# Products of rounded operands that take their columns in four turns of four, in a two-block transformer kernel

## The chip, the cores and the metric

The kernel runs on one core of a Trainium2 chip. The metric is the device time of one execution in microseconds. The engines are called by the profile's names: PE is the matrix engine (PEld its weight loads, which overlap its products), DVE the vector engine, ACT the scalar engine, POOL the general one, SP the one that issues the transfers.

## The reference, cut to what matters

256 tokens of width 1024 pass through two blocks in float32. The first block has latent attention, a state space, cross attention and a convolved gated feed-forward; the second has two layers of a gated feed-forward, a mixer with three branches, and another gated feed-forward. Nearly all arithmetic is in dense products with weights that are read once:

```
x = x + 0.5 * ((silu(h @ w1) * (h @ w3)) @ w2)          # four times, w1 and w3 1024 x 2816, w2 2816 x 1024
proj = h @ w_in[l]                                       # 1024 x 5632, two layers
merged = gate_0 * (y_sb @ w_sb) + gate_1 * (y_ret @ w_ret) + gate_2 * (y_pool @ w_pool)
x = x + merged @ w_out[l]
```

## The kernel before, in words

A float32 product is made of three products of rounded operands. `split` writes a value's high part (type float32r, by ACT) and the rest (float32r, by DVE); names that end in h and l are these parts (`wh`, `wl` of the weights, `gh`, `gl` of the gated values), and `h` is the normed input, in the two parts. `mm3` adds high by high, high by low and low by high into one PSUM bank. Products that aren't of such operands (transposes, attention, the state space) stay plain float32.

There are two forms. In `proj`, the down products and `merge_out` (tiles `pr`, `up`, `acc`) the tokens are the 128 columns of the stationary operand and 512 columns of weights stream through (some `pr` have 256, 160 or 384). In `proj_T` (tiles `pt`) the weights are stationary and both token tiles stream, 256 columns: the moving operand is a view `p t c` of two runs of 128. In `h` these two runs lie 512 elements apart, since `norm_T` lays a tile out as token tile, block, column (`t k c`); `split_pairs` does the same for the gated values of a first chunk. The output bank is written in the same order as the columns stream.

All instructions are recorded first, with estimated costs, and `Program.issue` gives each engine its order by a list schedule. What depends on what is found in `add`: two accesses to a tile depend on each other where `region` says that they overlap. `region` gives the box from an access's first to its last element of a row. PSUM banks count as whole. The schedule's own estimates are not used as times in this text.

All `mm` calls go through line 463, all transposes through line 488, ACT, DVE and POOL operations through line 379.

Of the kernel before, what the change touches and what calls it, by code (L numbers as in the profile page):

```python
# [18 lines left out]
D = 1024  # L19
# [23 lines left out]
def region(ap):  # L43
    """The partitions and the elements of a row that an access path may touch."""
    (row, parts), *free = ap.ap
    p, f = divmod(ap.offset, row)
    lo = f + sum(min(0, s * (n - 1)) for s, n in free)
    hi = f + sum(max(0, s * (n - 1)) for s, n in free) + 1
    return p, p + parts, lo, hi


def overlap(a, b):
    return a[0] < b[1] and b[0] < a[1] and a[2] < b[3] and b[2] < a[3]


def covers(a, b):
    return a[0] <= b[0] and b[1] <= a[1] and a[2] <= b[2] and b[3] <= a[3]


class Op:  # L60
    """An instruction to come: its engine, its call and its estimated time."""
# [7 lines left out]
class Program:  # L69
    """Records instructions with their data's order and issues them by a list schedule.  # L70

    Per engine, the instruction that is ready and comes first by priority goes next, as long
    as the rest of the program can still run in the order of an earlier schedule within the
    tile pools. The priorities are start times of the schedule that runs from the end.
    """

    ENGINES = ("pe", "act", "dve", "pool", "sp")
    # time from the end of an instruction to the start of one on another engine that waits for it
# [19 lines left out]
    def tile(self, t, tags, whole=False):  # L98
        """Makes a tile known: the pools it takes room in, and if any two accesses keep their order."""
        name = t.tensor.name  # L100
        self.tags[name] = tags
        if whole:
            self.whole.add(name)
        return t

    def add(self, eng, call, cost, reads, writes, kind=""):
        op = Op(eng, call, cost, kind)
        # the vector engine's second port to SBUF is Pool's only one
# [4 lines left out]
        for aps, w in ((reads, False), (writes, True)):  # L113
            for ap in aps:
# [5 lines left out]
                r = (0, 1, 0, 1) if name in self.whole else region(ap)  # L120
# [23 lines left out]
    def backward(self, order):  # L144
        """Latest start times, from a schedule that runs from the end, later instructions of order first."""
# [42 lines left out]
    def forward(self, prio, base):  # L188
        """A schedule by priority; base is an order that keeps within the pools."""
# [32 lines left out]
        def room(i, full):  # L222
            """The tiles that op i takes into use, or None when there is no room for them."""
# [126 lines left out]
class Engine:  # L350
    """An engine's calls, recorded with their cost."""
# [33 lines left out]
class Ctx:  # L385
    """Pools, constants, and the blocks shared by all layers."""
# [43 lines left out]
    def weights(self, w, n0, n):  # L430
        """w[:, n0:n0+n] as the two float32r parts of a product, per 128-row block a list of (hi, lo)."""
# [25 lines left out]
    def mm(self, ps, lhsT, rhs, start=True, stop=True):  # L457
        n, m = size(rhs), size(lhsT)
        if rhs.dtype == F32:
            ns = 2 * max(2 * n / 2.4 * min(1.0, 0.4 + m / 160), 107.0 * m / 128) + 5  # L460
        else:
            ns = max(n, 64) / 2.4 + 2.5
# [3 lines left out]
    def mm3(self, ps, x, w, start, stop):  # L466
        """ps (+)= x.T @ w, the small product of the low parts left to float32's rounding."""
        self.mm(ps, x[0], w[0], start, False)
        self.mm(ps, x[0], w[1], False, False)
        self.mm(ps, x[1], w[0], False, stop)  # L470

    def mm_rows(self, ps, xs, ws, start, stop):
        """ps[i] (+)= sum over k of xs[k].T @ ws[i][k], the products with the low parts of x last."""
# [23 lines left out]
    def split(self, src, hi, lo, scale=None):  # L497
        """Splits float32 data into two float32r parts, scaled by a constant or per partition."""
# [14 lines left out]
    def transposes(self, src, name="tr"):  # L513
        """[128, 128 n] to a bank with the n blocks transposed."""
# [11 lines left out]
    def load_gain(self, src, kind="load"):  # L526
        """A gain vector of 1024, on all partitions."""
# [5 lines left out]
    def norm_rows(self, halves, g):  # L533
        """rmsnorm of [128, 1024] rows given as two halves."""
        ss = self.sm("ss", 2)
        xs = [self.w("xs") for _ in range(2)]
        for b in range(2):
            junk = self.w("junk")
            # D is an even power of two: the scale is exact
# [10 lines left out]
    def norm_T(self, tiles, g):  # L550
        """rmsnorm of 256 rows, transposed and split: per half of the width (hi, lo), each [128, 2, 4, 128]."""
        out = []
        for b in range(2):
            pair = [self.prog.tile(self.hpool.tile([128, 1024], F32R, tag="h", name="h"), ("h",)) for _ in range(2)]
            out.append([v.rearrange("p (t k c) -> p t k c", t=2, k=4) for v in pair])
# [6 lines left out]
    def split_tokens(self, ps, dst, t):  # L562
        """Splits [128, 4 * 128] into the columns of token tile t of dst."""
# [3 lines left out]
    def norm_x(self, gain):  # L567
        """The norm of both token tiles of x, for the products to come."""
# [10 lines left out]
    def proj(self, w, n0, n, x=None, rows=False):  # L579
        """x.T @ w[:, n0:n0+n], per token tile; with rows one tile after the other."""  # L580
# [19 lines left out]
    def proj_T(self, w, n0, x=None):  # L600
        """w[:, n0:n0+256].T @ x for all tokens: two blocks of 128 rows in a bank."""
# [14 lines left out]
    def merge_out(self, m, scale, w):  # L616
        """x += (scale * m).T @ w, m as four tiles of two 128-row blocks of all tokens."""
# [16 lines left out]
    def swiglu(self, w1, w3, w2):  # L634
        """x += 0.5 * (silu(h w1) * (h w3)) w2."""
# [22 lines left out]
    def conv_swiglu(self, w_up, w_down, cw, cb):  # L658
        """x += (silu(g) * v) w_down with [g | v] the causal convolution of h w_up along the tokens."""
# [39 lines left out]
    def feed_forward(self, w1, w3, w2, gate_rows, gate, scale):  # L699
        """x += scale * gate(h w1, h w3) w2, by chunks of the inner width.  # L700

        The first chunk takes the token tiles one after the other, as the norm hands them over."""
# [43 lines left out]
    def gate_proj(self, w, n0, bias=None):  # L746
        """Gate of one branch, two blocks of 128 rows to a tile; with half the bias, tanh of half the logits."""
# [14 lines left out]
    def branch(self, y, w, gate, m, plus_one):  # L762
        """m + gate * (w.T @ y), into the gate's tiles when m is None."""
# [10 lines left out]
    def head_sums(self, src, heads, dim):  # L774
        """Sums of squares over the last axis of [128, heads, dim]; src may lie in PSUM."""
# [6 lines left out]
    def head_norm(self, src, heads, dim):  # L782
        """1 / rms over the last axis of [128, heads, dim]; src may lie in PSUM."""
        return self.rstd(self.head_sums(src, heads, dim), heads, dim)

# [1 line left out]
    def rope_tables(self):  # L787
        """cos and sin of positions * inv_freq, [128, 2, 16] each, from the reduced angles."""
# [12 lines left out]
    # 2 pi in parts of few bits, so that their products with the turns are exact  # L801
    PI2 = (6.28125, 0.0019340515136718750, 1.2556659e-06)

    def reduce_angle(self, ang, shift):
        """ang - 2 pi k, k = round(ang / 2 pi + shift)."""
# [20 lines left out]
    # The state space runs in chunks of 4 steps, a step's number being 4 a + b, with the inputs and the  # L826
    # outputs in the order (b, a). With s the state before a chunk and d the factor of a step (complex):
    #   output b of the chunk = sum over b' <= b of (C d^(b - b') B) u[b'] + (C d^b) g,  g = d s
    #   g of the next chunk   = d^4 g + sum over b of (d^(4 - b) B) u[b]
    # and in a frame that turns with the angle of d^4 the second is a scan with a real decay.  # L830

    def ssm_setup(self):
        """Powers of the factors, the angles of whole chunks, and the input and output maps."""
# [28 lines left out]
        # k - w with k = round(w + 1/4)  # L862
# [8 lines left out]
        # powers 0..4 of the factors  # L871
# [4 lines left out]
        # (factor - 1) / lambda  # L876
# [15 lines left out]
        # its products with the powers 4, 3, 2, 1, 0  # L892
# [15 lines left out]
    def ssm_maps(self, h):  # L908
        """Maps of state tiles 8h .. 8h + 8, block diagonal by the two groups of a tile."""
# [4 lines left out]
        def product(x, y, signs, powers, name):  # L914
            """x (real, imaginary), [128, i, c], by powers of y [128, z, k, i]; per part and four tiles [128, i, k, 32]."""
# [23 lines left out]
        # C[1] holds the negative imaginary part  # L939
# [15 lines left out]
        # cos and sin of the angles of 1..64 chunks  # L955
# [16 lines left out]
    def ssm_half(self, h):  # L972
        """The outputs of state tiles 8h .. 8h + 8."""
# [44 lines left out]
    def ssm_gelu(self):  # L1018
        # 2 gelu(y) = y (1 + tanh(sqrt(2 / pi) (y + 0.044715 y^3)))
# [11 lines left out]
    def ssm_glu(self):  # L1031
        """y * sigmoid(y @ w_glu + b_glu), with the width on the partitions."""
# [23 lines left out]
    def softmax(self, s, heads, scale):  # L1056
        """Over the last axis of [128, heads, n] in a bank."""
# [13 lines left out]
    def cross_T(self, src, g):  # L1071
        """Per-head rmsnorm of [128, 4 * 128] rows, transposed per head."""
# [31 lines left out]
    def split_pairs(self, ps, dst, t):  # L1104
        """Splits [128, n * 128] into token tile t's part of each (hi, lo) of dst, two blocks to one."""
        for i, d in enumerate(dst):
            q = size(d[0]) // 2
            self.split(ps[:, i * 256:i * 256 + q], *(z[:, t * q:t * q + q] for z in d))

    def pair_T(self, ys):  # L1110
        """Accessor for [128, 2 * 256] tiles that hold two 128-row blocks of all tokens."""
        return lambda k: tuple(v[:, (k % 2) * 256:(k % 2) * 256 + 256].rearrange("p (t c) -> p t c", t=2) for v in ys[k // 2])

    def tile_T(self, ys):
        """Accessor for the tiles of split_pairs."""
        return lambda k: tuple(v.rearrange("p (t k c) -> p t k c", t=2, c=128)[:, :, k % 2, :] for v in ys[k // 2])

    def mla_latents(self, t, cq, ckv, g, out):
        """Norms of the latents, transposed and split; rotated shared key part per token tile."""
# [8 lines left out]
        # shared key part: its sum of squares and its rotation, gains folded into the tables  # L1128
# [9 lines left out]
    def fold_rope(self, sn, cs, gb):  # L1138
        """Rotation tables with the gains of the rotated dims folded in, per token tile."""
# [20 lines left out]
    def mla_heads(self, qs, kv, lat, gq, gk):  # L1160
        """Four heads: norms, rotation, causal softmax, values: [128, 2 * 256], split."""
# [23 lines left out]
        # first token tile: own keys only; later keys of the own tile get the mask added  # L1185
# [401 lines left out]
```

## Time and profile before

| | |
|---|---|
| time, median of 3 runs | 1622.44 us (1622.29 to 1624.53) |
| span of the profiled execution | 1619.3 us |
| instructions | 28502 |
| PE busy, products | 1589.3 us, 98%, 11126 records |
| PEld busy, weight loads | 1455.3 us, 90% |
| DVE, ACT, POOL busy | 1019.0, 843.1, 134.9 us |
| HBM read | 284.88 MB, 177 GB/s over the span |
| granted PE clock | 0.998 of full |

The span is the time from the first to the last instruction of one profiled execution; the time of a run lies some 3 us above it. A product's duration in the profile runs from its start to the modelled end of its last column, so products that follow each other closely overlap; how fast they go is read from starts, or from a stretch's length over its count. A plain float32 product leaves two records, one of rounded operands one.

### The profile page before, as it was taken

The numbers are of one execution on the slowest core, as the hardware profiler recorded it, in microseconds if no ns is written. First come the engines' busy times: TensorE is split into PE (matmuls) and PEld (weight loads), VectorE is DVE, ScalarE is ACT, GpSimd is POOL, SyncE is SP. The second block draws the span as 40 slices with busy tenths as digits, with TensorE's granted clock in tenths as the row PEclk, the third lists the DMA queues.
The fourth block names the chain that finished last, engine by engine and source line by source line (L and its number), as shares of the span: only waits on it lengthen the run. The fifth ranks groups of instructions, "written<-read, shape, count | busy, mean of one in ns | idle before, by whom it ended". The sixth has DMA issues, their size and how long they took to land.

```text
span 1619.3 us, 28502 instructions
## 1 busy us (share of the span) xinstructions
PE 1589.3 (98%) x11126; PEld 1455.3 (90%) x11126; DVE 1019.0 (63%) x1759; ACT 843.1 (52%) x1746; POOL 134.9 (8%) x276
## 2 busy tenths in 40 slices
PE   7999999999999999999999999999999999999998
PEld 6889989899989999889998999899998899989997
DVE  6678797787676545755657554665457556574543
ACT  6984554665555434555446443454345554464431
POOL 4554500000000000000000000000000000000000
PEclk9999999999999999999999999999999999999999
DMA  8731464665557575454647666475654546475650
GB/s 258 232 104 53 148 208 130 221 202 176 184 171 248 170 228 183 145 181 137 195 138 234 195 197 193 142 243 169 224 182 146 180 137 196 137 236 194 197 181 26
DMA packets 214374, 288.30 MB, mean 178 GB/s; under 512 B 13792, under 2 KB 170080, under 8 KB 214240
## 3 DMA queue, kind: packets, MB, share of 16 engines
q1 hardware_dynamic: 214240, 286.49, 55.6%
q8 instruction: 87, 1.43, 0.4%
q14 instruction: 47, 0.39, 0.1%
HBM read 284.88 MB, written 1.05 MB: 177 GB/s over the span
## 4 chain that ended last, share of the span: by engine, by line
PE 91%; DVE 4%; ACT 2%; DMA 2%; issue 1%; POOL 0%; SPq 0%; POOLq 0%; DVEq 0%; ACTq 0%
PE pt L463 50%; PE acc L463 22%; PE pr L463 7%; PE up L463 7%; PE tr L488 2%; DVE wl L379 1%; ACT wh L379 1%; PE yb L463 1%; DMA x<-in_x_dram 0%; DVE sbp L379 0%; DVE pm L379 0%; PE rs L463 0%; DMA raw<-in_w_mem_kv_dram 0%; PE glu L463 0%; ACT sqh L379 0%
## 5 line engine op out<-in xcount | busy, mean ns | idle before, releaser
L379 DVE TENSOR_TENSOR wl<-raw,wh 128x512 fp32r<-128x512 f32 x1045 | 661.3, 685 | 210.3 <-ACT wh L379 189.5
L463 PE MATMUL pt<-h,wh 128*128 128x256 f32 x4224 | 758.4, 282 | 0.1
L379 ACT CAST wh<-raw 128x512 fp32r<-128x512 f32 x1045 | 580.5, 618 | 158.4 <-DMA raw<-in_w_in_dram 48.1
L463 PEld LDWEIGHTS pt<-h,wh 128*128 128x128 f32 x4224 | 650.3, 188 | 3.4 <-ACT gate L379 0.3
L463 PE MATMUL pt<-h,wl 128*128 128x256 f32 x2112 | 593.2, 281 | 0.0
L463 PEld LDWEIGHTS pt<-h,wl 128*128 128x128 f32 x2112 | 397.7, 188 | 0.2 <-issue 0.2
L463 PE MATMUL acc<-wh,gh 128*128 128x512 f32 x440 | 173.7, 395 | 0.0
L463 PE MATMUL acc<-wh,gl 128*128 128x512 f32 x440 | 173.2, 394 | 0.0
L463 PE MATMUL acc<-wl,gh 128*128 128x512 f32 x440 | 173.2, 394 | 0.0
L463 PE MATMUL pr<-wh,h 128*128 128x512 f32 (+2 forms) x480 | 134.6, 362 | 2.1 <-ACT h L379 1.5
L379 ACT CAST gh<-sg 128x512 fp32r<-128x512 f32 x47 | 29.1, 620 | 151.5 <-DVE sg L379 151.5
L463 PE MATMUL up<-wh,h 128*128 128x512 f32 x320 | 102.0, 397 | 0.0
L463 PEld LDWEIGHTS pr<-wh,h 128*128 128x128 f32 x480 | 85.5, 189 | 17.2 <-ACT h L379 1.9
L463 PEld LDWEIGHTS acc<-wh,gl 128*128 128x128 f32 x440 | 82.6, 188 | 19.5
L463 PEld LDWEIGHTS acc<-wl,gh 128*128 128x128 f32 x440 | 82.6, 188 | 18.1
L463 PEld LDWEIGHTS acc<-wh,gh 128*128 128x128 f32 x440 | 82.6, 188 | 18.0
L379 POOL TENSOR_SCALAR s<-ss 128x1 f32<-128x1 f32 x20 | 9.9, 494 | 1059.1 <-ACT junk L379 1059.0
L379 DVE TENSOR_TENSOR sg<-sg,pt 128x512 f32<-128x512 f32 x36 | 24.7, 687 | 114.9 <-PE pt L463 114.9
L379 ACT ACTIVATE sg<-pt 128x512 f32<-128x512 f32 x36 | 21.6, 599 | 135.3 <-PE pt L463 135.3
L463 PE MATMUL pr<-wl,h 128*128 128x512 f32 (+2 forms) x240 | 86.5, 361 | 0.5 <-DVE wl L379 0.5
L463 PEld LDWEIGHTS up<-wh,h 128*128 128x128 f32 x320 | 59.7, 188 | 13.8
L379 ACT ACTIVATE junk<-x 128x512 f32<-128x512 f32 x36 | 22.8, 632 | 87.1 <-DVE x L379 80.9
(346 smaller groups left out, 1665.0 us busy)
## 6 DMA issues: line engine op xcount, KB each, us to landing
raw<-in_w_ffn_dram SPq DMA_DIRECT2D x264, 512.0 KB, 5.0
raw<-in_w_in_dram SPq DMA_DIRECT2D x124, 512.0 KB, 4.9
raw<-in_w_up_dram SPq DMA_DIRECT2D x44, 512.0 KB, 4.9
raw<-in_w_out_dram SPq DMA_DIRECT2D x24, 512.0 KB, 4.1
raw<-in_w_down_dram SPq DMA_DIRECT2D x22, 512.0 KB, 4.4
raw<-in_w_mem_kv_dram SPq DMA_DIRECT2D x8, 512.0 KB, 5.2
raw<-in_w_branch_ret_dram SPq DMA_DIRECT2D x8, 512.0 KB, 3.8
raw<-in_w_o_mla_dram SPq DMA_DIRECT2D x4, 512.0 KB, 4.7
```

Of the source, the lines that this page charges most:

```text
L379: self.prog.add(self.name, lambda: getattr(self.eng, op)(**kw), self.cost(op, kw), list(aps.values()), writes, "fast" if self.name == "dve ...
L463: self.prog.add("pe", lambda: self.nc.tensor.matmul(ps, lhsT=lhsT, rhs=rhs, start=start, stop=stop), ns, [lhsT, rhs], [ps])
L488: self.prog.add("pe", lambda: self.nc.tensor.transpose(out, src, ident), 109, [src, ident], [out])
```

## The change

Every product with a float32r moving operand gets its moving operand and its output through `turns`: the n columns are seen as n/16 groups of 16, each of four fours. The product takes the first four columns of every group, then the second four of every group, then the third, then the fourth. Operand and output are walked in the same order, so each result lands in its old column. For this the columns must be one evenly stepped row: `norm_T`, `split_pairs` and `tile_T` now lay tiles out as block, token tile, column (`k t c`), so both token tiles of a block lie side by side, 256 elements in one run, and ACT and DVE write each tile of 128 x 512 as four runs of 128 elements 256 apart.

With this layout the boxes of the two token tiles would overlap, so `region` now also gives a mask of the 32-element pieces that an access really touches and whether it fills its box; accesses overlap only where masks meet, and one covers another only if it fills its box. The rest of the full diff takes out comments and docstrings.

```diff
     lo = f + sum(min(0, s * (n - 1)) for s, n in free)
     hi = f + sum(max(0, s * (n - 1)) for s, n in free) + 1
-    return p, p + parts, lo, hi
+    at = {f}
+    for s, n in free:
+        at = {a + s * i for a in at for i in range(n)}
+    mask = 0
+    for q in {a // 32 for a in at}:
+        mask |= 1 << q
+    return p, p + parts, lo, hi, mask, len(at) == hi - lo
 def overlap(a, b):
-    return a[0] < b[1] and b[0] < a[1] and a[2] < b[3] and b[2] < a[3]
+    return a[0] < b[1] and b[0] < a[1] and a[2] < b[3] and b[2] < a[3] and bool(a[4] & b[4])
 def covers(a, b):
-    return a[0] <= b[0] and b[1] <= a[1] and a[2] <= b[2] and b[3] <= a[3]
+    return a[5] and a[0] <= b[0] and b[1] <= a[1] and a[2] <= b[2] and b[3] <= a[3]
...
+    TURNS = 4
+
+    def turns(self, ap):
+        if len(ap.shape) == 3:
+            ap = ap.rearrange("p t c -> p (t c)")
+        return ap.rearrange("p (l a e) -> p a l e", a=self.TURNS, e=4)
+
     def mm(self, ps, lhsT, rhs, start=True, stop=True):
         n, m = size(rhs), size(lhsT)
+        if rhs.dtype == F32R:
+            ps, rhs = self.turns(ps), self.turns(rhs)
...
     def norm_T(self, tiles, g):
-            out.append([v.rearrange("p (t k c) -> p t k c", t=2, k=4) for v in pair])
+            out.append([v.rearrange("p (k t c) -> p t k c", t=2, k=4) for v in pair])
...
     def split_pairs(self, ps, dst, t):
         for i, d in enumerate(dst):
             q = size(d[0]) // 2
-            self.split(ps[:, i * 256:i * 256 + q], *(z[:, t * q:t * q + q] for z in d))
+            self.split(ps[:, i * 256:i * 256 + q].rearrange("p (k c) -> p k c", c=128),
+                       *(z.rearrange("p (k t c) -> p t k c", t=2, c=128)[:, t] for z in d))
     def tile_T(self, ys):
-        return lambda k: tuple(v.rearrange("p (t k c) -> p t k c", t=2, c=128)[:, :, k % 2, :] for v in ys[k // 2])
+        return lambda k: tuple(v.rearrange("p (k t c) -> p t k c", t=2, c=128)[:, :, k % 2, :] for v in ys[k // 2])
```

Most of the program keeps its order. PE's order at the second block's mixer, where the last small product of the pooling branch (`py`) is followed by the gates (`pt`, weights `wh`, `wl` stationary, `h` streaming), before:

```order
L488 MATMUL tr<-par,ry 128x128 x8
L463 MATMUL py<-pdT,wp 128x256 x2
L463 MATMUL pt<-h,wh 128x256 x2
L463 MATMUL pt<-h,wl 128x256
L463 MATMUL pt<-h,wh 128x256 x2
L463 MATMUL pt<-h,wl 128x256
```

The same place of the changed kernel:

```order
L504 MATMUL tr<-par,ry 128x128 x8
L479 MATMUL py<-pdT,wp 128x256 x2
L479 MATMUL pt<-h,wh 128x4x16x4 x2
L479 MATMUL pt<-h,wl 128x4x16x4
L479 MATMUL pt<-h,wh 128x4x16x4 x2
L479 MATMUL pt<-h,wl 128x4x16x4
```

Nothing moved there; the shape alone is new. In the first block, some 35 us after the start, the order of PE does change. There the latents of the attention (`cq`, `ckv`) are transposed and multiplied while products of `h` are at hand. Before:

```order
L463 MATMUL pr<-wl,h 128x512
L463 MATMUL pr<-wh,cqh 128x384
L488 MATMUL tr<-par,ckv 128x128 x2
L463 MATMUL pr<-wh,h 128x512
L463 MATMUL pr<-wl,cqh 128x384
L463 MATMUL pr<-wh,h 128x512
L463 MATMUL pr<-wh,cql 128x384
L463 MATMUL pr<-wh,cqh 128x384
```

The same place of the changed kernel:

```order
L479 MATMUL pr<-wl,h 128x4x32x4
L479 MATMUL pr<-wh,h 128x4x32x4 x2
L479 MATMUL pr<-wl,h 128x4x32x4
L504 MATMUL tr<-par,ckv 128x128 x2
L479 MATMUL pr<-wh,h 128x4x32x4 x2
L479 MATMUL pr<-wl,h 128x4x32x4
L479 MATMUL pr<-wh,h 128x4x32x4
L504 MATMUL tr<-par,ckv 128x128 x2
L479 MATMUL pr<-wh,h 128x4x32x4 x2
L479 MATMUL pr<-wl,h 128x4x32x4
L479 MATMUL pr<-wh,cqh 128x4x24x4
```

The products of `cqh` moved behind those of `h` and behind both transposes of `ckv`.

## Rows read from the trace of the kernel before

**Rows 1.** The page: span, busy times, and the chain that ended last by line.
```profile
span 1619.3 us, 28502 instructions
PE 1589.3 (98%) x11126; PEld 1455.3 (90%) x11126; DVE 1019.0 (63%) x1759; ACT 843.1 (52%) x1746; POOL 134.9 (8%) x276
...
PE pt L463 50%; PE acc L463 22%; PE pr L463 7%; PE up L463 7%; PE tr L488 2%; DVE wl L379 1%; ACT wh L379 1%; PE yb L463 1%; DMA x<-in_x_dram 0%; DVE sbp L379 0%; DVE pm L379 0%; PE rs L463 0%; DMA raw<-in_w_mem_kv_dram 0%; PE glu L463 0%; ACT sqh L379 0%
```

**Rows 2.** Busy time by stretch: bounds, length, engines with counts, granted clock, DMA share.
```profile
0.00:310.00 310.00, 288.06 (x2251) 261.58 (x2252) 237.32 (x446) 197.42 (x500) 101.69 (x206) 0.99 0.54 165
300.00:1600.00 1300.00, 1298.57 (x8867) 1191.89 (x8866) 779.50 (x1310) 649.12 (x1251) 31.21 (x64) 1.00 0.57 182
```

**Rows 3.** Pieces of the chain that ended last: start, length in us, what.
```profile
744.63 90.70 PE pt L463 x768
...
734.79 5.66 PE pr L463 x48
...
1590.35 22.30 PE acc L463 x96
...
1051.74 18.57 PE up L463 x80
```

**Rows 4.** Six-microsecond stretches of the gates: PE, PEld, DVE, ACT, POOL, clock, DMA.
```profile
757.00:763.00 6.00, 6.00 (x53) 6.00 (x52) 2.77 (x5) 3.28 (x7) 0.00 (x0) 1.00 1.00 317
763.00:769.00 6.00, 6.00 (x53) 6.00 (x52) 1.96 (x4) 2.95 (x7) 0.00 (x0) 1.00 0.14 49
...
805.00:811.00 6.00, 6.00 (x53) 6.00 (x52) 5.67 (x10) 2.77 (x5) 0.00 (x0) 1.00 0.94 283
...
823.00:829.00 6.00, 6.00 (x53) 6.00 (x52) 2.12 (x4) 2.86 (x6) 0.00 (x0) 1.00 0.03 12
```

**Rows 5.** Plain float32 on PE: timeline rows, then durations (minimum/median/maximum, ns).
```profile
704.31 0.60 PE L488 MATMUL tr<-par,z 128*128 128x128 f32 x4
...
743.60 1.03 PE L463 MATMUL py<-pdT,wp 128*128 128x256 f32 x4
...
L488 PE MATMUL tr<-par,z x24: 270/272/332, 704.3 to 1273.7; 128*128 128x128 f32 x24
...
L463 PE MATMUL py<-pdT,wp x8: 379/379/382, 743.6 to 1310.6; 128*128 128x256 f32 x8
```

**Rows 6.** Products of 160 columns: two timeline rows, then their count in the kernel.
```profile
28.18 0.28 PE L463 MATMUL pr<-wl,h 128*128 128x160 f32 x1
...
33.21 0.27 PE L463 MATMUL pr<-wl,h 128*128 128x160 f32 x1
...
L463 PE MATMUL pr<-wh,h 128*128 128x160 f32 x32 | 5.5, 274 | 0.0
L463 PE MATMUL pr<-wl,h 128*128 128x160 f32 x16 | 4.3, 275 | 0.0
```

**Rows 7.** Groups of products by form: count, busy us, mean ns, idle before.
```profile
L463 PE MATMUL pt<-h,wh 128*128 128x256 f32 x4224 | 758.4, 282 | 0.1
L463 PE MATMUL pt<-h,wl 128*128 128x256 f32 x2112 | 593.2, 281 | 0.0
L463 PE MATMUL acc<-wh,gh 128*128 128x512 f32 x440 | 173.7, 395 | 0.0
...
L463 PE MATMUL pr<-wh,h 128*128 128x512 f32 x320 | 104.9, 402 | 2.1 <-ACT h L379 1.5 <-ACT wh L379 0.6
L463 PE MATMUL up<-wh,h 128*128 128x512 f32 x320 | 102.0, 397 | 0.0
...
L463 PE MATMUL acc<-wh,mth 128*128 128x512 f32 x96 | 38.1, 397 | 0.0
```

**Rows 8.** ACT copies of 256 elements: fully scattered output, and one run.
```profile
L379 ACT COPY yp<-yt x4: 643/644/677, 194.3 to 225.0; 128x256 f32<-128x256 f32 x4
...
L379 ACT COPY vsb<-pr x4: 348/359/368, 704.5 to 1271.0; 128x256 f32<-128x256 f32 x4
```

More of the change, by code (lines that the diff above doesn't have):

```diff
@@ L119, in add @@
                     op.tiles.append(name)
-                r = (0, 1, 0, 1) if name in self.whole else region(ap)
+                r = (0, 1, 0, 1, 1, True) if name in self.whole else region(ap)
                 log = self.log[name]
```

## The prediction

> **What bounds the kernel now.** I read the page first, then busy time by stretch, then the chain, then single stretches of PE. The page says that PE is busy 98% of the span and that 50 + 22 + 7 + 7 = 86% of the chain that ended last are the products `pt`, `acc`, `pr` and `up` [rows 1], all of rounded operands. From 300 to 1600 us PE misses 1.4 of 1300 us, while DVE is busy 60%, ACT 50% and the DMA engines 57% [rows 2]. So nothing but the rate of PE's products can move the time much. Outside that stretch PE waits 310 - 288 = 22 us [rows 2].
>
> A busy PE says little about its pace, so I divide long pieces of the chain by their counts [rows 3]. 768 products of 256 columns take 90.70 us: 118.1 ns each. 96 products `acc` of 512 columns take 22.30 us: 232.3 ns each; `up` gives 18.57 / 80 = 232.1. The difference, 114.2 ns for 256 more columns, is 0.446 ns a column. The granted clock is 1.00 there [rows 2], the 2.4 GHz level, whose period is 0.417 ns. So a streamed column costs 7% more than a clock: about one clock is lost in 15 columns.
>
> Where is it lost? Plain float32 products don't lose it. Four records of `py` stand in 1.03 us and one lasts 0.379, so they are (1.03 - 0.379) / 3 = 217 ns apart, for 256 columns; four transposes of 128 columns are (0.60 - 0.272) / 3 = 109 ns apart [rows 5]. These take twice 256 and twice 128 clocks, 213 and 107, and some 3 ns. At half the reading rate a clock is a clock. Nor is it other engines: in four six-microsecond stretches of the gates, with the DMA share at 1.00, 0.14, 0.94 and 0.03 and DVE busy between 1.96 and 5.67 us, PE starts the same 53 products [rows 4]. Nor is it a break in the operand's addresses: `pt` reads two runs of 128, 512 elements apart, at 118.1 ns; 48 `pr` products of 256 columns in one run take 5.66 us, 117.9 ns each [rows 3]. What is left is the reading or writing of one 4-byte element per clock, in address order. That order is what the change alters.
>
> **The change part by part.** *Pace of the products.* From the groups [rows 7] and the recorded order I count 7248 products of 256 columns (4224 + 2112 `pt` of `h`; 672 more `pt` with other inputs, 192 `pr`, 48 `glu`) and 2592 of 512 (1320 + 288 `acc`, 480 `up`, 504 `pr`). The 84 of 384 and 160 columns I leave out. At today's paces they are 7248 x 118.1 + 2592 x 232.2 = 856 + 602 = 1458 us. The four lines hold 86% of 1619.3, about 1390 us on the chain: 95% of what a product gains or loses reaches the end.
>
> No row shows a product that takes its columns in fours, so the price is bounded. Below: 512 columns can't go under what 512 clocks cost today, the 217 ns of `py`. For 256 there is a second floor, the weight load of 128 columns ahead of each. Products of 160 columns show it: 48 exist, and from the second to the last but one are 45 steps in 33.21 - 28.18 = 5.03 us, 112 ns each [rows 6], though 160 columns at 0.446 are 71. The transposes with the same load manage 109 [rows 5]. I take 111 as the new pace of 256 columns, nearer to the 112 of the same operand type. If all of the loss goes: 7248 x 7.1 = 51 us and 2592 x 15.2 = 39 us, together 91; at 95%, 86 us. With 109 and 217 it would be (66 + 39) x 0.95 = 100 us. Above: each of the 63 steps to the next four in 256 columns (127 in 512) costs a clock, which is the first rival.
>
> Why do I take the gain? Contiguous reading loses one clock in about 15 columns, so the loss repeats at about the 16 columns that make up one group of `turns`. In the old order three of four steps from one four to the next stay inside a group; in the new order none does. A break of addresses costs nothing that shows: `pt` with a break is 0.2 ns slower than `pr` without, under half a clock. If neighbouring fours in one group hinder each other, the new order frees them.
>
> The Trainium skill (TensorE: Matmul & The Clock Gate, Back-to-back issue gap) gives n / 2.4 + 2.5 ns for a product alone, 109 and 216 ns. The trace disagrees for these operands, 118.1 and 232.2, and the rows decide; by the formula taken as a floor the sum would be 8.9 x 7248 + 16.2 x 2592 = 107 us, 101 on the path.
>
> *Layout.* ACT and DVE write `h` as four runs of 128 in place of one of 512, 36 times each. Copying 256 elements to wholly scattered places takes 644 ns against 359 for one run [rows 8], at most 1.1 ns a break, so three breaks are 3 ns, 0.2 us in all. Both engines have 40% to spare. I put zero.
>
> *Order.* The exact regions move rows of PE in the first block, in the 310 us that hold the 22 us of waiting [rows 2]. Of 10,300 PE rows some 200 stand elsewhere. A gain or loss of up to 5 us is my estimate, a quarter of that waiting; I put zero.
>
> *What is late next.* DVE's 780 us in 1300 [rows 2] would be in some 1215: 64%. ACT 53%, DMA 61%. Weight loads, busy 92% of that stretch, go to about 98%: they are the floor named above.
>
> Sum: 1619.3 - 86 = 1533 for the span. The median lies 3.1 us above the profiled span, so 1622.4 - 86 = 1536 us.
>
> **The rivals.** *Steps cost a clock (slower).* If reading from a new group, or writing the bank in pieces of four, costs PE one clock a step, 256 columns take 109 + 63 x 0.417 = 135 ns and 512 take 217 + 127 x 0.417 = 270. That is 7248 x 17 + 2592 x 38 = 222 us more: 1844 us; if today's loss stays on top, 1950. It turns at 7.1 / 63 = 0.11 ns a step: above, the kernel is slower. For it: the one break in `pt` can't resolve 0.11 ns, and it is a single long jump on the reading side alone; no row has a broken output. Against it: a full clock for that break would make `pt` 0.4 ns slower than `pr`, and 0.2 is seen.
>
> On this side stands the Trainium skill (Advanced Engine Details and Errata, Memory Cachelines): SBUF lines of 16 bytes, at full speed when accesses stay in a line, and PSUM lines of 8 bytes, where any pattern that isn't contiguous slows products significantly, though pairs should be together for best throughput. The fours keep lines of both sizes whole. By the SBUF half nothing changes, by the stricter PSUM half this rival holds; no row so far has such an output.
>
> *The rate belongs to the operand (no change).* If PE is handed these operands at 2.25 columns a ns however they lie, the paces stay 118 and 232 and the time 1622, give or take the order's few us. For it: the loss is the same in four kinds of stretch and in two layouts. Against it: all these read neighbours one after the other, so none tests it.
>
> *Part of the loss goes.* Half of it: 43 us, 1579 us. For it: a loss of one clock in 15 isn't exactly a period of 16, so it may have two sources.
>
> **How the numbers follow.** The forecast, 1515 to 1560 us by itself (100 us saved and 5 from the order; or two thirds of the gain), has 0.50. Part of the loss, 1560 to 1619, has 0.14. No change has 0.12, and steps that cost, 1626 to 1950, 0.24; a measurement of this kernel tells about 0.2%, 3 us, from no change. So faster 0.64, same 0.12, slower 0.24. The range starts at 1515 and must reach past no change into the mild end of the slower case to leave out two in ten: 1650, which is a price of some 0.15 ns a step.
>
> **What would show it.** In the profile after: the 768 gate products in 85 us (90.70 now), the 96 `acc` in 20.8 (22.30 now); PEld at some 95% of the span; the DVE and ACT writes of `h` unchanged. Gates at 118 ns again mean that the rate belongs to the operand; above it, that steps cost. If `acc` reaches 217 and `pt` stays at 118, the weight loads were already the bound of `pt`, and only 37 us come. If PE's waits before 310 us grow past 27, the order took something back. The prediction is wrong if a step costs over 0.11 ns.

## The result, and the profile after

| | before | after |
|---|---|---|
| time, median of 4 runs each | 1622.66 us (1622.29 to 1624.53) | 1603.47 us (1602.01 to 1607.41) |
| span of the profiled execution | 1619.3 us | 1601.1 us |

The ratio is 0.9885, 95% interval 0.987 to 0.9901: faster by 19.2 us. The forecast was 86 us faster. The page of the changed kernel, in the lines that answer to [rows 1] (span, PE's and other engines' busy time, the chain that ended last by line):

```profile
span 1601.1 us, 28476 instructions
...
PE 1558.5 (97%) x11126; PEld 1436.8 (90%) x11126; DVE 1023.9 (64%) x1759; ACT 841.3 (53%) x1748; POOL 133.1 (8%) x276
...
PE pt L479 47%; PE acc L479 19%; PE pr L479 8%; PE up L479 7%; PE tr L504 2%; DMA raw<-in_w_in_dram 2%; DVE wl L385 1%; ACT wh L385 1%; DVE x L385 1%; DMA raw<-in_w_ffn_dram 1%; PE yb L479 1%; POOL rs L385 1%; DVE cT L385 1%; DVE xB L385 0%; ACT L385 0%
```

PE lost 31 us of busy time (1589.3 to 1558.5), yet the span lost 18. The four product lines hold 81% of the chain (86% before), and transfers and small operations of DVE, ACT and POOL have come onto it. So PE now waits where it did not. Two readings settle how much is pace and how much is waiting. First the pace, from pieces of the chain of the changed kernel (start, length in us, what), to be set against [rows 3]:

```profile
730.66 5.53 PE pr L479 x48
...
740.39 88.19 PE pt L479 x768
...
859.24 10.87 PE up L479 x48
...
1572.80 21.70 PE acc L479 x96
```

88.19 / 768 = 114.8 ns for 256 columns (118.1 before), 21.70 / 96 = 226.0 ns for 512 (232.3), and `up` agrees with 10.87 / 48 = 226.5 (232.1). The 85 and 20.8 us that the prediction wanted were not reached, but both moved. Then the busy time by stretch of the changed kernel (bounds, length, PE, PEld, DVE, ACT, POOL with counts, granted clock, DMA share, GB/s), to be set against [rows 2] and [rows 4]:

```profile
0.00:310.00 310.00, 283.59 (x2228) 258.85 (x2229) 238.62 (x437) 194.72 (x492) 102.46 (x206) 0.97 0.53 163
300.00:1590.00 1290.00, 1280.41 (x8928) 1182.99 (x8926) 784.85 (x1322) 646.87 (x1256) 28.88 (x65) 1.00 0.58 185
...
750.00:756.00 6.00, 6.00 (x55) 6.00 (x54) 4.12 (x7) 3.81 (x7) 0.00 (x0) 1.00 1.09 350
...
762.00:768.00 6.00, 6.00 (x55) 6.00 (x54) 3.91 (x7) 3.34 (x7) 0.00 (x0) 1.00 0.15 46
...
798.00:804.00 6.00, 6.00 (x55) 6.00 (x54) 6.00 (x11) 2.22 (x4) 0.00 (x0) 1.00 0.69 203
```

These stretches of the gates show 55 products in six microseconds where [rows 4] show 53 (a stretch also counts the products under way at its start), again whatever DVE, ACT and the transfers do. In the first 310 us PE misses 26.4 us (22 before) and its mean clock is 0.97 (0.99). Behind 300 us it misses 9.6 us of 1290, where it missed 1.4 of 1300.

### The profile page after: what moved, and what is told of

Its sections match the earlier page's. It is cut to its first block, busy times and chain, and to the rows that moved or that the text cites. A ratio compares the mean times of both kernels' runs of the same rounds, so it can differ in the third digit from the quotient of the medians.

```text
span 1601.1 us, 28476 instructions
## 1 busy us (share of the span) xinstructions
PE 1558.5 (97%) x11126; PEld 1436.8 (90%) x11126; DVE 1023.9 (64%) x1759; ACT 841.3 (53%) x1748; POOL 133.1 (8%) x276
## 4 chain that ended last, share of the span: by engine, by line
PE 85%; DVE 6%; ACT 3%; DMA 3%; issue 1%; POOL 1%; SPq 0%; POOLq 0%; DVEq 0%; ACTq 0%
PE pt L479 47%; PE acc L479 19%; PE pr L479 8%; PE up L479 7%; PE tr L504 2%; DMA raw<-in_w_in_dram 2%; DVE wl L385 1%; ACT wh L385 1%; DVE x L385 1%; DMA raw<-in_w_ffn_dram 1%; PE yb L479 1%; POOL rs L385 1%; DVE cT L385 1%; DVE xB L385 0%; ACT L385 0%
## 5 line engine op out<-in xcount | busy, mean ns | idle before, releaser
L385 DVE TENSOR_TENSOR wl<-raw,wh 128x512 fp32r<-128x512 f32 (+1 forms) x1045 | 658.3, 688 | 189.1 <-ACT wh L385 187.7
L479 PE MATMUL pt<-h,wh 128*128 128x256 f32 x4224 | 735.3, 277 | 0.0
L479 PEld LDWEIGHTS pt<-h,wh 128*128 128x128 f32 x4224 | 642.2, 188 | 3.2 <-issue 0.7
L479 PE MATMUL pt<-h,wl 128*128 128x256 f32 x2112 | 584.3, 277 | 0.0
L479 PE MATMUL acc<-wh,gh 128*128 128x512 f32 x440 | 170.3, 387 | 0.0
L385 POOL TENSOR_SCALAR s<-ss 128x1 f32<-128x1 f32 x20 | 5.3, 267 | 901.5 <-ACT junk L385 901.4
```

The lines of the kernel that those rows point to most:

```text
L385: self.prog.add(self.name, lambda: getattr(self.eng, op)(**kw), self.cost(op, kw), list(aps.values()), writes, "fast" if self.name == "dve ...
L479: self.prog.add("pe", lambda: self.nc.tensor.matmul(ps, lhsT=lhsT, rhs=rhs, start=start, stop=stop), ns, [lhsT, rhs], [ps])
```

## The experiments

The two parts of the change can be taken apart. The walk (`turns`) sets the pace; the layout with its exact `region` changes which operations depend on each other, and through the list schedule the order. Pace is given below as the length of one piece of the chain over its count, so that the reader can see both; a kernel without its own number of runs was timed once beside one run or more of the kernel before.

### The order without the turns, and the turns without the order

**a_noturn** is the changed kernel with its layout and order, the columns in one row:

```diff
-            ps, rhs = self.turns(ps), self.turns(rhs)
+            ps, rhs = (v.rearrange("p t c -> p (t c)") if len(v.shape) == 3 else v for v in (ps, rhs))
```

> The changed kernel with its layout and its order of instructions, but each product takes its columns in one row, as before. Theory 1 (the new order costs time by itself): the paces are 118 and 232 ns again, PE's waits stay as in the changed kernel, and the time is 1622 + 12 to 20 = 1634 to 1642 us. Theory 2 (the order is innocent, faster products outrun the weights' transfers): the time is that of the kernel before, 1619 to 1626 us.

Measured: 1636.4 us against 1621.18 of the kernel before (4 and 7 runs), ratio 1.0093 (1.0076 to 1.011). The order alone is 15.2 us slower. Its stretches of PE, the part before 310 us, the part behind 300 us, and three at a granted clock of 0.50:

```profile
0.00:310.00 310.00, 284.11 (x2208) 257.75 (x2209) 237.83 (x437) 193.50 (x489) 102.86 (x206) 0.97 0.51 161
300.00:1580.00 1280.00, 1272.31 (x8658) 1165.58 (x8657) 770.26 (x1300) 638.16 (x1240) 30.13 (x66) 1.00 0.57 185
...
100.24:107.07 6.83, 5.60 (x25) 4.94 (x26) 3.39 (x6) 4.35 (x9) 0.00 (x0) 0.50 0.54 161
151.44:158.27 6.83, 5.01 (x26) 4.25 (x23) 4.50 (x6) 1.99 (x8) 2.74 (x3) 0.50 0.01 2
175.33:178.74 3.41, 3.40 (x11) 3.05 (x12) 3.41 (x7) 2.10 (x6) 0.00 (x0) 0.50 0.73 209
```

**b_oldorder** keeps turns and layout, but records the accesses of the new tiles by the boxes that they had in the old layout, so the schedule comes out in the old order:

```diff
+def region_as(ap, k):
...
+    at = [(a // 128 % 2) * 128 * k + a // 256 * 128 + a % 128 for a in at]
+    return p, p + parts, min(at), max(at) + 1, 1, True
```

> The changed kernel's turns and layout, with dependences computed so that every engine gets the order of the kernel before. Theory 1: the paces of the changed kernel (115 and 226 ns) without its waits, 7248 x 3.4 + 2592 x 5.8 = 40 us, at 95% 38 us under the kernel before: 1581 to 1589 us. Theory 2: the waits come back although the order is the old one: 1600 to 1606 us.

Measured: 1591.09 us against 1621.18 (4 and 7 runs), ratio 0.9818 (0.9803 to 0.9833). It beats the kernel before by 30.1 us, where the changed kernel beat it by 19.2, and every engine has the order of the kernel before, row for row. It lies 2 us above the 1581 to 1589 that were expected of the paces alone. Its gates stand below. Ahead of 310 us it has 13.65 us at a clock of 0.50, in three stretches of which the longest is this:

```profile
171.83:178.66 6.83, 6.83 (x51) 5.12 (x50) 1.29 (x2) 4.81 (x13) 4.83 (x6) 0.50 0.52 171
```

**exact_regions** is the kernel before with nothing but the new dependence test, in the old layout and without turns:

```diff
...
 def overlap(a, b):
-    return a[0] < b[1] and b[0] < a[1] and a[2] < b[3] and b[2] < a[3]
+    return a[0] < b[1] and b[0] < a[1] and a[2] < b[3] and b[2] < a[3] and bool(a[4] & b[4])
...
```

> The kernel before with the exact regions alone: old layout, one row, no turns. Every engine's order is that of the changed kernel. If the regions' new order is what costs: the time of a_noturn, 1633 to 1640 us. If the new layout costs (four runs of 128 in the writes of h, one run of 256 in the reads): 1620 to 1626 us.

Measured: 1637.02 us against 1622.82 (4 and 7 runs), ratio 1.0086 (1.007 to 1.0103): 14.2 us slower. Every engine's order is that of the changed kernel, row for row. So the slower order comes from the sharper test, and the layout as such costs nothing that these runs can tell: a_noturn has it and exact_regions has not, 15.2 and 14.2 us with intervals that overlap.

Where does the order lose? What PE waited for, over the whole kernel before (engine, line waited for: us in total, times, longest):

```profile
PE tr L488 <- DVE xs L379: 10.8, 2, 10.6
PE yb L463 <- DVE sg L379: 3.9, 1, 3.9
PE pr L463 <- ACT h L379: 1.5, 1, 1.5
```

And the same view of the changed kernel:

```profile
PE tr L504 <- DVE xs L385: 9.6, 4, 8.3
PE up L479 <- ACT h L385: 8.6, 5, 2.9
PE mo L479 <- ACT p L385: 3.4, 1, 3.4
PE kT L479 <- DVE cT L385: 2.9, 3, 1.4
```

The waits of `up` for ACT's cast of `h` (8.6 us) and of `mo` for `p` (3.4 us) are new. One of the five waits of `up`, in the timeline of the changed kernel on ACT, ahead of the second block's last feed-forward (start, length, what, in brackets the idle time before it and what ended it):

```profile
850.58 0.19 ACT L385 ACTIVATION_READ_ACCUMULATOR junk<-x 128x1 f32 x1
852.85 0.62 ACT L385 CAST wh<-raw 128x512 fp32r<-128x512 f32 x1 [2.08 <-DMA raw<-in_w_ffn_dram]
853.37 0.58 ACT L385 CAST h<-tr 128x512 fp32r<-128x512 f32 x1
```

And on its PE:

```profile
850.10 1.03 PE L504 MATMUL tr<-par,xs 128*128 128x128 f32 x8
854.00 0.49 PE L479 MATMUL up<-wh,h 128*128 128x512 f32 x1 [2.87 <-ACT h L385]
...
855.20 0.63 PE L479 MATMUL up<-wh,h 128*128 128x512 f32 x1
855.62 0.63 PE L479 MATMUL up<-wl,h 128*128 128x512 f32 x1
```

The transposes are all issued together, and ACT's order has a weight cast ahead of the cast of `h`. That weight is still in transfer, so ACT stands 2.08 us in front of it with the `h` that PE needs queued behind. In the kernel before, ACT takes `h` first at this place, and its PE goes from `tr` to `up` without a wait:

```profile
857.62 0.57 ACT L379 CAST h<-tr 128x512 fp32r<-128x512 f32 x1
858.48 0.62 ACT L379 CAST wh<-raw 128x512 fp32r<-128x512 f32 x1 [0.29 <-DMA raw<-in_w_ffn_dram]
```

A second cost comes behind such waits. The starts at 855.20 and 855.62 are 0.42 us apart, not 0.226. Three stretches of the changed kernel with its granted clock, the number behind POOL's (columns as above; the one at 100.44 starts 0.2 us behind the end of the wait of `mo`, the one at 148.23 0.1 us behind a wait of `kT` of 1.35 us):

```profile
100.44:103.85 3.41, 3.41 (x17) 3.08 (x17) 1.13 (x3) 2.93 (x6) 0.00 (x0) 0.50 0.74 192
148.23:155.06 6.83, 5.44 (x36) 4.27 (x36) 4.95 (x6) 2.05 (x8) 3.19 (x3) 0.50 0.01 2
...
854.79:858.20 3.41, 3.41 (x10) 2.56 (x9) 2.68 (x6) 1.81 (x4) 1.10 (x2) 0.50 0.11 37
```

0.50 is the 1.2 GHz level. In the same three stretches the kernel before has a clock of 1.00. Ahead of 310 us its only stretch at 0.50 has 3.41 us, from 219.77 us, and stands shortly behind its wait of `yb` of 3.9 us.

### Reading or writing

Both kernels have the old order (they are built on b_oldorder) and turn one side alone. **c_read** turns the operand and fills the bank from its first column to its last; **d_write** reads the operand from first to last and turns only the bank:

```diff
-            ps, rhs = self.turns(ps), self.turns(rhs)
+            rhs = self.turns(rhs)                                            # c_read
+            ps = self.flat(ps).rearrange("p (a l e) -> p a l e", a=self.TURNS, e=4)
...
+            ps = self.turns(ps)                                              # d_write
+            rhs = self.flat(rhs).rearrange("p (a l e) -> p a l e", a=self.TURNS, e=4)
```

> As b_oldorder, but only the moving operand is read in four turns; the output is written in one row, so results land in other columns. If the loss lies in reading the operand: 115 and 226 ns. If it lies in writing the bank: 118 and 232 ns or more.

> As b_oldorder, but only the output is written in four turns; the operand is read in one row, so results land in other columns. If the loss lies in reading the operand: 118 and 232 ns, or more if broken writes cost something of their own. If it lies in writing the bank: 115 and 226 ns.

Measured: c_read 1590.47 us and d_write 1621.38 us, against 1621.18 of the kernel before and 1591.09 of b_oldorder on the same chip. Their chains, c_read:

```profile
1190.23 21.04 PE acc L489 x93
...
1287.30 88.37 PE pt L489 x768
```

d_write:

```profile
744.37 90.70 PE pt L489 x768
835.07 21.59 PE acc L489 x93
```

And b_oldorder:

```profile
1190.37 21.04 PE acc L485 x93
...
1287.39 88.37 PE pt L485 x768
```

The read side has the whole gain, to the last digit. Writing the bank in pieces of four columns costs nothing and gives nothing here.

### Other walks

All keep the old order and correct columns, and change `TURNS`, the piece `e` or the order of the view: two, eight and sixteen turns of four (t2, t8, t16), four turns of eight (e8), eight turns of two (t8e2), fours by turns from either half (far2), and one row from the last column to the first (m_rev):

```diff
-    TURNS = 4
+    TURNS = 8                                                               # t8
...
-        return ap.rearrange("p (l a e) -> p a l e", a=self.TURNS, e=4)
+        return ap.rearrange("p (l a e) -> p a l e", a=self.TURNS, e=8)      # e8
+        return ap.rearrange("p (h l e) -> p l h e", h=2, e=4)               # far2
...
+            ps, rhs = ps[:, ::-1], rhs[:, ::-1]                             # m_rev
```

> As b_oldorder with two turns in place of four: the fours of a turn lie 8 columns apart. Theory S (spacing: fours that follow each other hinder the more the nearer they lie): paces between one row and four turns, 116 to 117.5 and 228 to 231 ns, 1600 to 1612 us. Theory W (the loss comes from meetings of the two reading streams of PE, moving operand and weight load): no order by spacing is foretold; any pace from 110 to 118.

> As b_oldorder with eight turns: fours 32 columns apart. Theory S: under the 114.9 and 226.7 ns of four turns, 111 to 113.5 and 218 to 224 ns, 1560 to 1580 us. Theory W: no further gain that follows from the spacing, about 115 and 227 ns, 1588 to 1596 us.

> As b_oldorder with four turns of eight columns: half of the steps from one four to the next go to a neighbour again. Theory S: half of the gain, 116.5 and 229.3 ns, 1604 to 1608 us. Theory W: not foretold, about 115 to 118 ns.

> Order of the kernel before; every product of rounded operands takes its columns from the last to the first, operand and output alike, in one row. Theory N (what counts is which lines of the operand follow each other): 118 and 232 ns, 1619 to 1625 us. Theory W (meetings with the weight load's reads, which keep their direction): another pace, by 1 ns or more in 256 columns.

> As b_oldorder with eight turns of two columns: the step is 16 columns as with four turns of four, but pieces are 8 bytes. If the step of 16 columns is what helps: 115 and 227 ns again. If pieces of four are needed: slower than one row, over 118 and 232 ns, by the rule that a visit to a line should use it.

> As b_oldorder with sixteen turns (eight where the columns don't divide): fours that follow each other lie 64 columns, 256 bytes, apart. Theory P (what hinders is a step that comes back to the same part of the memory, and a step of 128 bytes does): as bad as eight turns, 123 to 125 and 243 to 247 ns, 1684 to 1692 us. Theory D (the farther the step, the more it costs): clearly over eight turns, 128 ns or more, 1720 us or more. Theory S (the nearer, the worse) fell with t8.

> As b_oldorder, but the fours are taken in turn from the two halves of the columns: 0, n/2, 4, n/2 + 4 and so on, so every step is 512 or 1024 bytes there and a little less back. Theory P: each step out ends on the same part of the memory, as a step of eight turns does, each step back on the next part, so half of the loss of eight turns: 119 to 121 and 236 to 240 ns. Theory D: the worst of all, over 128 ns. If neither counts and only neighbours hinder each other: under 115 ns.

Measured, with the pace as length over count of a piece of each chain (768 gate products, and the `acc` in one piece):

| kernel | from one piece to the next | time, us | before on that chip | 256 columns, ns | 512 columns, ns |
|---|---|---|---|---|---|
| a_noturn (one row, new order) | 16 B | 1636.4 | 1621.18 | 90.78 / 768 = 118.2 | 10.43 / 45 = 231.8 |
| t2 | 32 B | 1622.0 | 1621.31 | 90.56 / 768 = 117.9 | 21.55 / 93 = 231.7 |
| b_oldorder (four turns) | 64 B | 1591.09 | 1621.18 | 88.37 / 768 = 115.1 | 21.04 / 93 = 226.2 |
| t8 | 128 B | 1686.02 | 1621.31 | 94.67 / 768 = 123.3 | 22.86 / 93 = 245.8 |
| t16 | 256 B | 1856.46 | 1622.97 | 104.50 / 768 = 136.1 | 25.88 / 93 = 278.3 |
| far2 | 512 or 1024 B, to and fro | 1733.26 | 1622.97 | 98.57 / 768 = 128.3 | 23.40 / 93 = 251.6 |
| e8 | 16 and 112 B by turns | 1616.76 | 1621.31 | 89.81 / 768 = 116.9 | 21.63 / 93 = 232.6 |
| t8e2 | 64 B, pieces of 8 B | 2870.97 | 1622.82 | 139.57 / 637 = 219.1 | 40.40 / 93 = 434.4 |

The rows of four of them, t2:

```profile
745.65 90.56 PE pt L485 x768
836.22 21.55 PE acc L485 x93
```

t8:

```profile
768.73 94.67 PE pt L485 x768
863.40 22.86 PE acc L485 x93
```

t16:

```profile
839.11 104.50 PE pt L486 x768
943.61 25.88 PE acc L486 x93
```

and t8e2:

```profile
1299.87 139.57 PE pt L485 x637
1439.43 40.40 PE acc L485 x93
```

m_rev took 1625.94 us (1622.82 before on that chip); its 768 gates take 90.80 us, 118.2 ns each as in a row, and its `acc` 21.76 / 93 = 234.0, some 2 ns more than in a row: the direction of the walk hardly matters. Of the others, only the step of 64 bytes beats the row by more than a nanosecond or so at both lengths. The theory that neighbouring fours hinder each other wants t8 to be at least as fast as four turns; it is 8 ns slower at 256 columns and 20 ns at 512. The theory that far steps cost fits 64 to 256 bytes, but not that a row at 16 bytes is slower than 64, nor that far2, with longer jumps than t16, is faster than it. And t16, which one theory put beside t8, costs 13 and 32 ns more than it. So none of the theories S, W, P and D fits all of these walks.

### The weight loads

**half_w** streams in one row, and all but the first and the last product of a sum take 64 of the 128 stationary columns, so the loads shrink; **half_w_turn** does so with the turns. Both have the old order.

```diff
+            if not (start or stop):
+                ps, lhsT = ps[0:64], lhsT[:, 0:64]
```

> Order of the kernel before, one row, no turns; but all products of a sum except the first and the last take 64 of their 128 stationary columns and fill half of the output, so half of the weights' columns is left out. Theory S (the moving operand alone): 118 and 232 ns stay. Theory W: half of the weights' reads, so half of the loss beyond 109.2 and 215.8 ns or less is left: 113 to 115 and 222 to 226 ns.

> b_oldorder with its four turns, but all products of a sum except the first and the last take 64 of their 128 stationary columns and fill half of the output, so half of the weights' columns is left out. If what is left of the loss under four turns comes from the weight load (its reads or its length): near 110 and 217 ns, about 1550 us. If not: 114 to 115 and 226 to 227 ns, 1580 to 1590 us.

Measured: half_w 1613.53 us (1621.31 before on that chip), half_w_turn 1584.29 (1622.82). The chain of half_w:

```profile
741.31 89.83 PE pt L487 x768
831.14 10.41 PE acc L487 x45
```

These are 117.0 and 231.3 ns; half_w_turn has 88.01 and 10.12 us for the same counts, 114.6 and 224.9. Half of the stationary columns is worth 7.8 us in a row and, beside b_oldorder's 30.1, 38.5 - 30.1 = 8.4 us with turns: about one nanosecond a product. That the smaller loads do matter where a load is the limit is shown by the products of 160 columns. They came every 112 ns in the kernel before [rows 6]; in half_w, 15 of them with 64 stationary columns lie between these two starts:

```profile
27.94 0.24 PE L487 MATMUL pr<-wl,h 128*64 128x160 f32 x1
...
29.06 0.24 PE L487 MATMUL pr<-wl,h 128*64 128x160 f32 x1
```

That is 1.12 us over 15, 75 ns each. So the experiment took the load away as a limit, and 256 columns hardly noticed. The cost of a column did not change either: (231.3 - 117.0) / 256 = 0.446 ns, as in the kernel before. So the loads are not what holds 256 columns at 118 or 115, and the loss per column is not a matter of how many weights are loaded beside it, as far as halving them can show. The half products also write half of the bank's partitions, so the nanosecond may belong to either.

## Why the prediction was wrong

The direction was right, the size was not: 19 us came of 86. Two of its steps failed, and the missing 67 us fall into three parts. The pace that came is 7248 x 3.3 + 2592 x 6.3 = 24 + 16 = 40 us of products, at the prediction's 95% 38 us; so 86 - 38 = 48 us are the pace. In the old order the turns gained 30.1 of these 38 us (b_oldorder), which leaves 8. An estimate places some 5 of them: b_oldorder has 13.65 - 3.41 = 10.2 us more at half clock than the kernel before, where half of the time is lost, and the prediction has no term for that. Most of the other 3 are its paces, 115.1 and 226.2 ns against the 114.8 and 226.0 of the changed kernel: 7248 x 0.3 + 2592 x 0.2 = 2.7 us. The new order took the 11 us between 30.1 and 19.2.

**The pace term was mis-sized, because its mechanism was guessed.** The step that failed is "If neighbouring fours in one group hinder each other, the new order frees them", and the choice that all of the loss goes. Of the 7.1 and 15.2 ns that were to go, 3.3 and 6.3 went: 46 and 41%. That is the rival "part of the loss goes", which put 1579 us without an order's cost. The mechanism is not borne out: three of four steps stay inside a group of 16 columns in a row, one of two with two turns, and none with four or with eight; two turns move nothing, and eight are slower than a row. The reading of a period of 16 columns out of "one clock in 15" had no row of its own, and no row distinguished it from another loss per column. Why a step of 64 bytes is better than 16 or 32, and what the rest of the loss is, stays open after these runs. What is shown is that the part that went is on the read side (c_read, d_write), and that halving the stationary columns takes about a nanosecond off a product and nothing off the cost of a column.

**The order was put at zero with 5 us either way; it costs 14 to 15 without the turns and 11 with them.** The estimate was a quarter of the waiting in the first 310 us. That waiting bounds what could be gained there, not what could be lost. The estimate also rests on PE's rows in the first block alone, while ACT's order changed as well, in the second block too (the cast at 852.85 above). In a_noturn PE's first feed-forward product starts at 301.2 us, in the kernel before at 290.9. These 10.3 us are waits and clock: a_noturn misses 25.9 us of PE before 310 us, 4 more than the kernel before, and has 17.07 us at half clock where that one has 3.41. The prediction's own sign, PE's waits growing past 27 us, did not show at 26.4, since a busy PE at half clock counts as busy. The spans of the two profiles, 1635.9 and 1619.3, differ by 16.6 us; the other 6.3 come behind that product, where the prediction looked for no change at all. There PE misses 7.7 us of 1280 in a_noturn and 1.4 of 1300 in the kernel before; `up` waits 5.5 us for `h` in a_noturn, in five places, and not once in the kernel before. Which entry of the schedule's priorities tips these casts was not tried.

**Steps that stood.** Only products of rounded operands have the loss, and the turns touch nothing else. It is no matter of other engines: 55 products in each of the three stretches of the gates, with a DMA share from 0.15 to 1.09. The layout costs next to nothing: DVE's writes of `h` average 686 ns (680 before), ACT's 585 (585), and one row runs at 118.2 as two runs did at 118.1. PEld is busy 1183 of 1290 us, 92% as before, not 98%. In the gates it was busy without a break before and after, 6.00 of 6.00 us, so its share can't tell whether it binds; half_w does, and there it doesn't bind 256 columns. The floor of 111 ns that the prediction put under them was reached by no run.

**The rival that a step costs a clock.** Its bank half is refuted: d_write's bank is in pieces, and it runs like the kernel before. The Trainium skill (Advanced Engine Details and Errata, Memory Cachelines) says that any pattern in PSUM that isn't contiguous slows products significantly; pieces of 16 bytes here do not, 118.1 and 232.2 ns. Its other half is real where the step is longer: from 64 to 256 bytes, 512 columns go from 226.2 to 278.3 ns, 52 ns over 127 steps, 0.41 ns each, and 256 columns from 115.1 to 136.1, 0.33 ns each of 63 steps: most of a clock of 0.417. The turning point lies between four turns and eight, and this change is on its good side by one doubling of the turns.

## What to carry to other kernels

When a loss is read as so much per column, don't take its removal at full size until a run moves it; here a step of 64 bytes returned four tenths, and 128 bytes made it worse. A sharper dependence test is a new schedule: cost it as a change of its own, or hold the order and change one thing, which was worth 11 us here. Look at the granted clock beside the busy time: here waits of PE of 1.35, 2.87 and 3.38 us were followed by stretches at half speed that count as busy.

## What the runs showed of the hardware that was not expected

- A visit to a 16-byte piece seems to cost about the same whether two of its four columns are taken or all four: t8e2 takes 219.1 / 128 = 1.71 ns for a piece of two columns, the row 118.2 / 64 = 1.85 for one of four, four turns 115.1 / 64 = 1.80. So pieces of 8 bytes nearly double the time, 2870.97 us. The bank was in pieces of 8 bytes as well, and which side costs was not tried, so this is not shown to be the operand's alone. The Trainium skill (Advanced Engine Details and Errata, Memory Cachelines) asks for at least two hits on a 16-byte line of SBUF; with two, a product took 219.1 ns here.
- The pace depends on the step and not steadily: 118.2, 117.9, 115.1, 123.3 and 136.1 ns for steps of 16 to 256 bytes, and 128.3 for jumps of 512 and 1024.
- The turned kernel in the old order gained only 1.0 us up to its first feed-forward product (289.9 against 290.9), and it has 13.65 us at half clock in the first 310 us where the kernel before has 3.41. The rest of it, 1328.4 to 1298.9 us, has the gain.
- Products of 160 columns came every 112 ns with 128 stationary columns and every 75 ns with 64. So the load of the stationary columns set their pace, and the moving columns set that of 256 and 512.
